# Opening of a two-layer encoder: modulation sums moved ahead of matrix products, one vector pass moved behind the low weights

## The chip, the cores and the metric

The kernel runs on one core of one Trainium2 chip. The metric is the time of one launch on the device, in microseconds (us); smaller is better. The engines of a core are TensorE (PE in the profile, with its weight loads as PEld), VectorE (DVE), ScalarE (ACT), GpSimd (POOL) and SyncE (SP), which here issues nearly all DMAs.

## The reference, cut to what matters

The whole computation is two layers of an encoder on 1024 tokens of width 1024 in float32. The change touches only what stands at the front of the first layer:

```
cond = jax.nn.silu(c)
mod = cond @ w_mod[l] + b_mod[l]
sh_a, sc_a, gt_a, sh_f, sc_f, gt_f = [m[:, None, :] for m in split_cols(mod, (D,) * 6)]
h = rms_norm(x, g_attn[l]) * (1 + sc_a) + sh_a
proj = h @ w_in[l]
```

Three groups of attention heads follow, an output projection, and a feed-forward part, all of it twice, and a last normalisation.

## The kernel before, in words

Products are made in "fp32r": a factor is split into a high part and a low part (`hh` and `hl` for the activations h, `whi` and `wlo` for weights), and three products high by high, low by high and high by low are added in PSUM. ACT makes the high part by a cast, DVE or POOL subtracts it to get the low part.

The width 1024 of h stands as eight chunks of 128 rows on the partitions, with the tokens along the free axis in two halves of 512. The opening (from line 816, `pin((pe, act, dve, sp), True)` among its first lines, up to the loop over the layers) works on the first half of the tokens in pairs of chunks. The attention part of `mod` (its columns for shift and scale) isn't ready beforehand: for each pair p it is made while the weights `w_mod` arrive, by the class `Mods`. Each pair reads two tiles `gm` of `w_mod`, rows 0 to 3 and rows 4 to 7 of eight blocks of 128 rows. The eight blocks are shared between two engines. DVE takes five or six of them (`m.add`), each as one multiply-add into the accumulator `ga` (128x512). PE takes the others directly (`m.col`), as four small matmuls of the gm block with the condition vector (`ps_m<-condT,gm`, 128x64; the profile counts each as two). `m.total(a)` then sums `ga` over the partitions with a column of ones (`ps_m<-onesr,ga`), for chunk a of the pair, and `m.finish(a)` lets DVE add the bias (`mod`) and form the scale (`gsc`). Only then can DVE scale the chunk (`nt`), ACT write its high part (`hh`), and DVE its low part (`hl`). For the first chunk of a pair in the first two pairs the scaling is done another way: `turned(n, rows)` multiplies the chunk of x by the row factors beforehand (`nt<-xt,rb`), and `h_turned` finishes it on ACT (`hh<-nt,mod,gsc`) and POOL (`ht`).

PE's main work beside this is `products(p, between)`: the chunks 2p and 2p+1 times the weights of the third head group (`wC`, loaded as `wst`, split by `w_high` on ACT and `low` on DVE), for four token blocks into four PSUM banks `ps_c`. It issues six passes of four 128x512 matmuls: high by high and high by low weights of the first chunk (`ps_c<-whi,hh`, `ps_c<-wlo,hh`), high by high of the second, low by high of both (`ps_c<-whi,hl`), and high by low weights of the second chunk. `between` is a list of functions, one called behind each pass. `a_first(u, q)` makes the chunks 2q and 2q+1 times the weights of the first head group (six matmuls `ps_ab`). `keep_busy(n)` issues n matmuls `ps_idle` that nobody reads, so that PE doesn't rest.

Loads of the opening go through SP's one queue in the order of the code: gm tiles (`gm_load`, three buffers), weight tiles `wst` (two buffers), blocks of x (`xn`). A load waits for its buffer, and those behind it wait with it.

What sets the order: within the opening PE, ACT, DVE and SP are pinned, so that each engine's instructions stand in the order in which the code calls them. POOL is not pinned, nor is what comes behind the opening: a scheduler places it. `skA<-skr`, a DMA that spreads a small bias table over 1 MB of device memory, belongs to that later part; its only reader here is `zv<-skA`, issued from 135.65 us on.

Of the kernel before, what the change touches and what calls it, by code (L numbers as in the profile page):

```python
# [76 lines left out]
def f32(ap):  # L77
    return ap.bitcast(F32)


def bc(ap, shape):
    return ap.to_broadcast(shape)
# [3 lines left out]
def trunk(ctx: ExitStack, tc, A, C, out):  # L86
# [115 lines left out]
    def mm3(ps, ah, al, bh, bl, first, last, **kw):  # L202
        pe.matmul(ps, ah, bh, start=first, stop=False, **kw)
        pe.matmul(ps, al, bh, start=False, stop=False, **kw)
        pe.matmul(ps, ah, bl, start=False, stop=last, **kw)
# [24 lines left out]
    def sub(out, a, b, eng=dve):  # L230
        eng.tensor_tensor(out=out, in0=a, in1=b, op=ALU.subtract)
# [328 lines left out]
    def x_load(half, j):  # L560
        t = stp.tile([P, D], F32, name="xn", tag="xn", bufs=4)
        r0 = half * H + j * P
        sp.dma_start(t, A["x"][0, r0 : r0 + P, :])
        return t

    def x_square(half, j, xn, r):
        junk = xt[:, 6:8, H:S]
        act.activation(
            junk, xn.rearrange("p (a b) -> p a b", a=2), AF.Square, accum_out=r[:, j : j + 1]
        )  # L570
# [43 lines left out]
    def turn_vecs(l, v):  # L614
        pst = psl.tile([P, 512], F32, name="pst", tag="mm")
        pe.transpose(pst[:, :72], v, ident[:72, :72])
        dve.tensor_copy(vecs[l], pst[:, :72])
# [5 lines left out]
    def gm_load(i, ks=(range(4),)):  # L623
        if i not in gms:
            gms[i] = stp.tile([P, 4, 2, 2 * P], F32, name="gm", tag="gm", bufs=3)
        for k in ks:
            r0 = (i % 2 * 4 + k.start) * P
            for g in range(2):
                c0 = g * 1024 + i // 2 * 2 * P
                rows = A["w_mod"][0, r0 : r0 + len(k) * P, c0 : c0 + 2 * P]  # L630
                sp.dma_start(
                    gms[i][:, k.start : k.stop, g, :], rows.rearrange("(k p) n -> p k n", p=P)
                )
# [55 lines left out]
    def turned(n, rows):  # L689
        t = stp2.tile([P, H], F32, name="nt", tag="nt", bufs=3)  # L690
        dve.tensor_tensor(out=t, in0=xt[:, n, 0:H], in1=rows, op=ALU.mult)
        return t

    def h_turned(n, xr):


        sh, sc = mods[0][:, n : n + 1], gsc[0][:, n : n + 1]
        act.activation(hh[:, n, 0:H], xr, AF.Identity, bias=sh, scale=sc)
        t = stp2.tile([P, H], F32, name="ht", tag="ht", bufs=1)
        pool.tensor_scalar(out=t, in0=xr, scalar1=sc, scalar2=sh, op0=ALU.mult, op1=ALU.add)  # L700
        return lambda: sub(hl[:, n, 0:H], t, f32(hh[:, n, 0:H]))

    def h_high(n, rows):
        t = stp2.tile([P, H], F32, name="nt", tag="nt", bufs=3)
        sh = mods[0][:, n : n + 1]
        dve.scalar_tensor_tensor(
            out=t, in0=xt[:, n, 0:H], scalar=gsc[0][:, n : n + 1], in1=rows,
            op0=ALU.mult, op1=ALU.mult,
        )
        act.activation(hh[:, n, 0:H], t, AF.Identity, bias=sh)  # L710
        return lambda: dve.scalar_tensor_tensor(
            out=hl[:, n, 0:H], in0=t, scalar=sh, in1=f32(hh[:, n, 0:H]),
            op0=ALU.add, op1=ALU.subtract,
        )

    def h_blocks(half, rows, ns, between=None):

        c = slice(half * H, (half + 1) * H)
        ts = {}
        for n in ns:  # L720
            t = ts[n] = stp2.tile([P, H], F32, name="nt", tag="nt", bufs=3)
            dve.scalar_tensor_tensor(
                out=t, in0=xt[:, n, c], scalar=gsc[0][:, n : n + 1], in1=rows,
                op0=ALU.mult, op1=ALU.mult,
            )
        for n, t in ts.items():
            act.activation(hh[:, n, c], t, AF.Identity, bias=mods[0][:, n : n + 1])
        for n, t in ts.items():
            dve.scalar_tensor_tensor(
                out=hl[:, n, c], in0=t, scalar=mods[0][:, n : n + 1], in1=f32(hh[:, n, c]),  # L730
                op0=ALU.add, op1=ALU.subtract,
            )
            if between:
                between()
                between = None

    def wc_stage(kp):
        st = stage()
        for dst, v in w_in_src(0, C_COLS, kp)(parts(st, 2)):
            sp.dma_start(dst, v)  # L740
        wcs.append(st)

    def c_first(n, passes=range(3)):

        wh, wl = wC[n // 2]
        first, last = n == 0, n == KC - 1
        for i in passes:
            h, w = ((hh, wh), (hl, wh), (hh, wl))[i]
            for t in range(T0):
                pe.matmul(  # L750
                    pssC[t], h[:, n, t * P : (t + 1) * P], w[:, n % 2],
                    start=first and i == 0, stop=last and i == 2, skip_group_check=True,
                )

    def products(p, between):

        n = 2 * p
        for a, i in ((n, 0), (n, 2), (n + 1, 0), (n, 1), (n + 1, 1), (n + 1, 2)):
            c_first(a, (i,))
            if between:  # L760
                between.pop(0)()

    def a_stage(u):
        ast.append(w_ab(0, EARLY_AB[u]))

    def a_high(u):

        st = parts(ast.pop(0), 2)
        hi, lo = (t[:, 6 - 2 * u : 8 - 2 * u, H:S] for t in (hh, hl))
        act.activation(hi, st, AF.Copy, scale=-0.125)  # L770
        return lambda: dve.scalar_tensor_tensor(
            out=lo, in0=st, scalar=-0.125, in1=f32(hi), op0=ALU.mult, op1=ALU.subtract
        )

    def a_first(u, p):

        for k in (2 * p, 2 * p + 1):
            n, c = 6 - 2 * u + k // 4, slice(H + k % 4 * P, H + k % 4 * P + P)
            mm3(
                pssA[u], hh[:, n, c], hl[:, n, c], hh[:, k, 0:H], hl[:, k, 0:H],  # L780
                k == 0, k == KC - 1,
            )
# [6 lines left out]
    def w_ab(l, oc):  # L789
        st = stage()  # L790
        c0 = oc * P if oc < 4 else 768 + (oc - 4) * P
        sp.dma_start(
            parts(st, KC), A["w_in"][l, :, c0 : c0 + P].rearrange("(k p) n -> p k n", p=P)
        )
        return st
# [23 lines left out]
    def keep_busy(n):  # L819

        for _ in range(n):
            pe.matmul(idle, identr, bc(identr[:, None, :], [P, 4, P]), start=True, stop=True)

    def w_high():
        st = wcs.pop(0)
        hi, lo = (wp.tile([P, 1024], F32R, name=n, tag="whl", bufs=8) for n in ("whi", "wlo"))
        wC.append((parts(hi, 2), parts(lo, 2)))
        act.copy(hi, st)
        return lambda: sub(lo, st, f32(hi))
# [32 lines left out]
    xr = [turned(0, rows)]  # L862
    rb = stp2.tile([P, H], F32, name="rb", tag="rb", bufs=2)
# [3 lines left out]
    m = Mods(0)  # L867
# [12 lines left out]
    first_low = next(lows)  # L880
    m.finish(0)
    low0 = h_turned(0, xr.pop(0))
    xr.append(turned(2, rb))
    m.total(1)
    m.finish(1)
    low1 = h_high(1, rb)
# [2 lines left out]
    second_low = next(lows)  # L889
    low1()  # L890
    second_low()
    gm_load(3)
    wc_stage(1)
    gm_load(4)
    a_stage(0)
    m = Mods(1)
# [3 lines left out]
    low()  # L900
    keep_busy(3)
    pssC = [psl.tile([P, 512], F32, name="ps_c", tag="mm") for _ in range(T0)]
    products(0, [lambda: None, lambda: None, lambda: m.col(3), lambda: None, lambda: m.col(6)])
    m.col(7)
    m.total(0)
    m.finish(0)
    low0 = h_turned(2, xr.pop(0))
    m.total(1)
    m.finish(1)
    low1 = h_high(3, rb)  # L910
    turn_vecs(1, v1)
    low0()
    low1()
    keep_busy(2)
    a_high(0)()
    gm_load(5)
    wc_stage(2)
# [4 lines left out]
    m = Mods(2)  # L922
    m.add(0, 1, 2)
    low = w_high()
    m.add(4, 5)
    low()
    m.add(6)
    pssA = [psl.tile([P, 512], F32, name="ps_ab", tag="mm") for _ in range(2)]
    products(1, [lambda: None, lambda: m.col(3)])
    a_first(0, 0)  # L930
    m.col(7)
    a_first(0, 1)
    m.total(0)
    m.total(1)
    m.finish(0)
# [2 lines left out]
    for j in (2, 3):  # L938
        xns[1].append(x_load(1, j))
    a_stage(1)  # L940
    h_blocks(0, rb, (4, 5))
    x_square(1, 0, xns[1][0], rxs[1])
    keep_busy(2)
    m = Mods(3)
    m.add(0, 1, 2)
    low = w_high()
# [24 lines left out]
    rb = stp2.tile([P, H], F32, name="rb", tag="rb", bufs=2)  # L971
# [37 lines left out]
    for l in range(2):  # L1009
# [861 lines left out]
        for n in range(-AHEAD - 1, N + 3):  # L1871
# [83 lines left out]
            m = n - 1 if n <= NC else n - 3  # L1955
# [572 lines left out]
        for u in range(NU):  # L2528
# [26 lines left out]
            if t < NB - 1:  # L2555
                continue
            m, half = {
                1: (0, 0), 2: (0, 0), 6: (0, 1), 7: (1, 1), 4: (1, 0), 5: (1, 1), 3: (0, 1),
            }[num]
# [25 lines left out]
        if last_layer:  # L2585
            blocks_ = [(1, j, nh) for j in range(4) for nh in range(2)]
            turned = [out_turn(*b) for b in blocks_[:7]]
# [106 lines left out]
```

## Time and profile before

| | before |
|---|---|
| median of three runs | 2370.83 us |
| the three runs | 2367.87, 2371.65, 2370.83 us |
| the profiled execution | 2369.28 us |
| its span, first to last instruction | 2367.5 us |
| mean granted TensorE clock over the span | 0.997 |
| PE busy | 2325.4 us |
| DVE busy | 1757.1 us |
| ACT busy | 1184.3 us |
| POOL busy | 778.0 us |

The profiled execution has a time of its own, 1.78 us over its span; sums from the trace are made against it. A row of the timeline has its start and its length in us, the engine, the operation, what it writes and reads, how many instructions were merged into it, and in brackets the idle time before it with what ended that. Starts on PE follow each other; the length of a matmul includes its way through the array, so that it overlaps the next one's start. A row of the stretches gives for each engine the busy time, then the clock granted to TensorE (1.00 is full), the share of the DMA engines' time and the bytes moved.

### The profile page before, as it was taken

What the parts mean: (1) busy time and instruction counts of PE and PEld (TensorE: products, weight loads), DVE (VectorE), ACT (ScalarE), POOL (GpSimd) and SP (SyncE); (2) the same over time, 40 slices, a digit from 0 to 9 for tenths busy, and PEclk for the clock granted to TensorE, in tenths of its full rate; (3) what the DMA queues carried; (4) which work ended last, traced back from release to release, by engine and by line L of the source; (5) the groups of instructions that cost most, each with busy time, mean ns of one, the idle gap of its engine ahead of it and who ended that gap; (6) DMA issues with size and microseconds to landing.
All of it is one profiled execution on the core that took longest, in us unless ns stands there. A gap on an engine that the chain in (4) does not pass through costs nothing.

```text
span 2367.5 us, 33491 instructions
## 1 busy us (share of the span) xinstructions
PE 2325.4 (98%) x11804; PEld 1959.8 (83%) x11804; DVE 1757.1 (74%) x2762; ACT 1184.3 (50%) x2262; POOL 778.0 (33%) x749
## 2 busy tenths in 40 slices
PE   9999999999999999999999999999999999999998
PEld 7888898888788888788888889988878888888886
DVE  6877998868867677595767689897796674537865
ACT  4423888845543333344633168896454434334443
POOL 1540446710344444100145124574005444430001
PEclk9999999999999999999999999999999999999999
DMA  8567406163445444785434861332634443339633
GB/s 290 172 204 222 135 21 195 46 214 98 130 137 165 156 138 151 218 244 173 155 102 134 245 186 28 92 103 96 216 98 134 154 149 103 98 109 291 213 120 112
DMA packets 307450, 358.02 MB, mean 151 GB/s; under 512 B 52029, under 2 KB 223901, under 8 KB 307281
## 3 DMA queue, kind: packets, MB, share of 16 engines
q1 hardware_dynamic: 290784, 346.26, 46.5%
q10 hardware_dynamic: 16128, 9.44, 1.5%
q8 instruction: 93, 1.52, 0.3%
q14 instruction: 77, 0.62, 0.1%
q0 software_dynamic: 368, 0.17, 0.0%
HBM read 270.84 MB, written 88.63 MB: 152 GB/s over the span
## 4 chain that ended last, share of the span: by engine, by line
PE 55%; DVE 5%; issue 4%; ACT 2%; DMA 2%; POOL 1%; SPq 0%; POOLq 0%; DVEq 0%; ACTq 0%
PE ps_w L49 23%; PE ps_d L49 15%; PE ps_o L49 4%; PE ps_ab L49 3%; PE pv L49 3%; PE T L49 2%; PE ps_v L49 2%; PE sC L49 2%; DMA wmt<-in_w_mod_dram 1%; DVE ws L49 1%; PE ps_c L49 1%; ACT pr L49 1%; DVE wpt L49 1%; DVE pt L49 0%; POOL ct L49 0%
## 5 line engine op out<-in xcount | busy, mean ns | idle before, releaser
L49 PE MATMUL ps_d<-wpt 128*128 128x512 f32 x1848 | 423.7, 390 | 1.0 <-ACT wpt L49 0.7
L49 PEld LDWEIGHTS ps_d<-wpt 128*128 128x128 f32 x1848 | 345.7, 188 | 74.3 <-issue 3.0
L49 POOL TENSOR_SCALAR pr<-pr,rs 128x1024 f32<-128x1024 f32 (+2 forms) x248 | 190.2, 781 | 186.3 <-DVE rs L49 168.9
L49 POOL TENSOR_TENSOR sg<-sg,u 128x512 f32<-128x512 f32 x82 | 118.4, 1445 | 347.7 <-ACT sg L49 221.6
L49 PE MATMUL pv<-pt,vs 128*128 128x256 f32 x1088 | 174.0, 296 | 14.2 <-DVE y L49 13.0
L49 ACT CAST wpt<-w 128x512 fp32r<-128x512 f32 x154 | 95.7, 621 | 182.2 <-PE ps_d L49 162.0
L49 DVE TENSOR_TENSOR pt<-T,pt 128x512 fp32r<-128x512 f32 x272 | 177.4, 679 | 7.1 <-ACT pt L49 5.7
L49 DVE SCALAR_TENSOR_TENSOR acc<-wmt,condT,acc 128x512 f32<-128x512 f32 (+1 forms) x98 | 115.9, 1189 | 79.9 <-DMA wmt<-in_w_mod_dram 79.4
L49 ACT CAST pt<-T 128x512 fp32r<-128x512 f32 x272 | 151.6, 585 | 42.4 <-PE T L49 41.0
L49 ACT COPY u<-ps_w 128x512 f32<-128x512 f32 x128 | 75.1, 587 | 192.9 <-PE ps_w L49 192.9
L49 POOL TENSOR_TENSOR wpt<-ws,wpt 128x512 fp32r<-128x512 f32 x80 | 111.1, 1390 | 181.5 <-ACT wpt L49 137.0
L49 DVE TENSOR_TENSOR wpt<-w,wpt 128x512 fp32r<-128x512 f32 x154 | 108.7, 706 | 81.3 <-ACT wpt L49 79.2
L49 PEld LDWEIGHTS pv<-pt,vs 128*128 128x128 f32 x1088 | 141.0, 189 | 27.0 <-DVE y L49 25.0
L49 PE MATMUL T<-identr,pr 128*128 128x128 f32 x1176 | 160.1, 273 | 0.8 <-DVE pt L49 0.4
L49 PEld LDWEIGHTS T<-identr,pr 128*128 128x128 f32 x1176 | 137.7, 140 | 15.8 <-issue 1.4
L49 ACT CAST wpt<-ws 128x512 fp32r<-128x512 f32 x176 | 107.7, 622 | 52.4 <-issue 23.0
L49 DVE TENSOR_TENSOR wpt<-graw,wpt 128x512 fp32r<-128x512 f32 x154 | 109.8, 713 | 16.6 <-ACT wpt L49 16.6
L49 DVE TENSOR_TENSOR wpt<-ws,wpt 128x512 fp32r<-128x512 f32 x96 | 82.5, 868 | 49.4 <-ACT wpt L49 49.1
L49 ACT CAST wpt<-graw 128x512 fp32r<-128x512 f32 x154 | 95.0, 617 | 46.9 <-DMA graw<-gpd 41.0
L49 DVE TENSOR_TENSOR ws<-wr 128x512 f32<-128x512 f32 x88 | 81.2, 923 | 49.9 <-POOL wpt L49 46.4
L49 DVE TENSOR_REDUCE rs<-sC 128x1 f32<-128x1024 f32 x88 | 107.4, 1220 | 12.4 <-PE sC L49 11.0
L49 PE MATMUL ps_w<-h22h,wpt 128*128 128x512 f32 x352 | 109.0, 391 | 2.7 <-ACT u L49 1.7
(310 smaller groups left out, 5937.1 us busy)
## 6 DMA issues: line engine op xcount, KB each, us to landing
wr<-in_w_gu_dram SPq DMA_DIRECT2D x92, 512.0 KB, 4.2
gpd<-sg SPq DMA_DIRECT2D x154, 256.0 KB, 4.3
graw<-gpd SPq DMA_DIRECT2D x76, 512.0 KB, 3.6
w<-in_w_down_dram SPq DMA_DIRECT2D x110, 256.0 KB, 5.0
wmt<-in_w_mod_dram SPq DMA_DIRECT2D x48, 512.0 KB, 5.7
qk<-qkd SPq DMA_DIRECT2D x44, 512.0 KB, 7.2
wst<-in_w_o_dram SPq DMA_DIRECT2D x32, 512.0 KB, 4.2
wmt<-in_w_mod_dram SPq DMA_DIRECT2D x64, 256.0 KB, 3.9
```

What stands on the lines that cost most here:

```text
L49: ins = op(*args, **kwargs)
```

## The change: what it does

Four things are rewritten in the opening of the first layer. The shared variable names below (`low0`, `low1`) are the functions that make the low parts later.

1. `turned(2, rb)` (one 128x512 multiply on DVE, `nt<-xt,rb`) leaves its place between the modulation sums of the first two chunks and stands behind the low part of the first weights.
2. In the first `products`, the last column (`m.col(7)`), both totals and both finishes are called behind the fifth pass instead of behind the sixth; `m.col(6)` moves one pass forward. One of the two `ps_idle` behind it is dropped.
3. For the pair of chunks 4 and 5, DVE's last row of the accumulator is added before the low weights are made, and both totals stand ahead of `a_first(0, 1)`.
4. The number of `ps_idle` ahead of the third `products` goes from two to three.

```diff
-    xr.append(turned(2, rb))
     m.total(1)
     m.finish(1)
     low1 = h_high(1, rb)
...
     second_low()
+    xr.append(turned(2, rb))
     gm_load(3)
...
-    products(0, [lambda: None, lambda: None, lambda: m.col(3), lambda: None, lambda: m.col(6)])
-    m.col(7)
-    m.total(0)
-    m.finish(0)
-    low0 = h_turned(2, xr.pop(0))
-    m.total(1)
-    m.finish(1)
-    low1 = h_high(3, rb)
+
+    def last_columns():
+        nonlocal low0, low1
+        m.col(7)
+        m.total(0)
+        m.finish(0)
+        low0 = h_turned(2, xr.pop(0))
+        m.total(1)
+        m.finish(1)
+        low1 = h_high(3, rb)
+
+    products(
+        0,
+        [
+            lambda: None, lambda: None, lambda: m.col(3), lambda: m.col(6), last_columns,
+            lambda: None,
+        ],
+    )
     turn_vecs(1, v1)
     low0()
     low1()
-    keep_busy(2)
+    keep_busy(1)
...
-    m.add(4, 5)
+    m.add(4, 5, 6)
     low()
-    m.add(6)
...
     a_first(0, 0)
     m.col(7)
-    a_first(0, 1)
     m.total(0)
     m.total(1)
...
     a_stage(1)
+    a_first(0, 1)
     h_blocks(0, rb, (4, 5))
     x_square(1, 0, xns[1][0], rxs[1])
-    keep_busy(2)
+    keep_busy(3)
```

How the rows stand on the engines follows; a difference has - for the order before and + for the order of the change.

On PE, in the first `products` (chunks 0 and 1, with the modulation of chunks 2 and 3 in `ps_m`):

```order
 L49 MATMUL ps_c<-whi,hh 128x512 x4
 L49 MATMUL ps_m<-condT,gm 128x64 x4
-L49 MATMUL ps_c<-whi,hl 128x512 x8
+L49 MATMUL ps_c<-whi,hl 128x512 x4
 L49 MATMUL ps_m<-condT,gm 128x64 x4
-L49 MATMUL ps_c<-wlo,hh 128x512 x4
+L49 MATMUL ps_c<-whi,hl 128x512 x4
 L49 MATMUL ps_m<-condT,gm 128x64 x4
 L49 MATMUL ps_m<-onesr,ga 128x64 x4
+L49 MATMUL ps_c<-wlo,hh 128x512 x4
 L49 MATMUL pst<-identr,v_150 128x72
-L49 MATMUL ps_idle<-identr 128x512 x2
+L49 MATMUL ps_idle<-identr 128x512
```

The totals (`ps_m<-onesr,ga`) moved ahead of the last pass `ps_c<-wlo,hh`, and one `ps_idle` is gone.

On PE, from the last column of the modulation of chunks 4 and 5 to the next `products`, before:

```order
L49 MATMUL ps_m<-condT,gm 128x64 x4
L49 MATMUL ps_ab<-hh 128x512
L49 MATMUL ps_ab<-hh,hl 128x512
L49 MATMUL ps_ab<-hl,hh 128x512
L49 MATMUL ps_ab<-hh 128x512
L49 MATMUL ps_ab<-hh,hl 128x512
L49 MATMUL ps_ab<-hl,hh 128x512
L49 MATMUL ps_m<-onesr,ga 128x64 x4
L49 MATMUL ps_idle<-identr 128x512 x2
L49 MATMUL ps_c<-whi,hh 128x512 x4
```

and in the change:

```order
L49 MATMUL ps_m<-condT,gm 128x64 x4
L49 MATMUL ps_m<-onesr,ga 128x64 x4
L49 MATMUL ps_ab<-hh 128x512
L49 MATMUL ps_ab<-hh,hl 128x512
L49 MATMUL ps_ab<-hl,hh 128x512
L49 MATMUL ps_ab<-hh 128x512
L49 MATMUL ps_ab<-hh,hl 128x512
L49 MATMUL ps_ab<-hl,hh 128x512
L49 MATMUL ps_idle<-identr 128x512 x3
L49 MATMUL ps_c<-whi,hh 128x512 x4
```

The six matmuls of `a_first(0, 1)` stood ahead of the totals and stand behind them now.

On SP, behind the last loads of the opening (`g` holds gains, `cst` rotary tables, `t` the bucket table; `xd<-xt` writes x back to device memory):

```order
-L49 DMA wst<-in_w_in_dram 128x8x128
-L49 DMA skA_91<-skr 512x1x512
-L49 DMA wst<-in_w_in_dram 128x8x128
+L49 DMA wst<-in_w_in_dram 128x8x128 x2
 L49 DMA g_532<-in_gq_ax_dram 128x6x64
 L49 DMA g_532<-in_gk_ax_dram 128x2x64
 L49 DMA cst<-const_rope_dram 128x128 x4
 L49 DMA t_544<-in_t_table_dram 32x6
+L49 DMA skA_91<-skr 512x1x512
 L49 DMA wst<-in_w_in_dram 128x8x128
```

The scheduler places the 1 MB `skA` behind the small tables now. Behind the opening no other row of any engine is moved.

## The prediction

> **What bounds the kernel now.** I read the busy times first, then the stretches around the change, then the timelines of PE and DVE there.
>
> ```profile
> PE 2325.4 (98%) x11804; PEld 1959.8 (83%) x11804; DVE 1757.1 (74%) x2762; ACT 1184.3 (50%) x2262; POOL 778.0 (33%) x749
> 41.45:43.77 2.32, 0.71 (x4) 0.28 (x3) 1.89 (x7) 0.77 (x2) 0.00 (x0) 1.00 1.10 381
> 43.77:48.10 4.33, 4.33 (x16) 3.63 (x17) 4.22 (x6) 4.30 (x7) 1.75 (x2) 0.61 0.83 264
> 90.00:150.00 60.00, 59.45 (x303) 48.93 (x302) 45.83 (x68) 23.54 (x53) 33.78 (x30) 1.00 0.56 153
> ```
>
> PE is busy 98% of the span, so a microsecond that PE gets back in the opening is worth a microsecond at the end, as long as nothing behind it is tied to something else: behind the opening (90 to 150 us) PE stands still for 0.55 us in 60. The opening has two visible losses. From 41.45 to 43.77 PE is busy for 0.71 us of 2.32, with `ps_idle` at that. From 43.77 to 48.10 PE is busy throughout, but its granted clock is 0.61 instead of 1.00: about 0.39 x 4.33 = 1.7 us of PE's work is lost to half clock. The DMA engines are full (share 1.10) in the first of these stretches, as in those ahead of it, so loads can't come earlier than they do.
>
> The timeline of PE, from the last pass of the first `products`:
>
> ```profile
> 26.71 1.17 PE L49 MATMUL ps_c<-wlo,hh 128*128 128x512 f32 x4
> 27.72 1.00 PE L49 MATMUL ps_m<-condT,gm 128*128 128x64 f32 x8
> 28.56 0.61 PE L49 MATMUL ps_m<-onesr,ga 128*128 128x64 f32 x4
> 29.42 0.66 PE L49 MATMUL ps_m<-onesr,ga 128*128 128x64 f32 x4 [0.26 <-DVE mod L49]
> 29.92 0.23 PE L49 MATMUL pst<-identr,v 72*128 72x72 f32 x1
> 29.95 0.71 PE L49 MATMUL ps_idle<-identr 128*128 128x512 f32 x2
> 30.50 1.17 PE L49 MATMUL ps_c<-whi,hh 128*128 128x512 f32 x4
> ...
> 33.24 1.17 PE L49 MATMUL ps_c<-whi,hh 128*128 128x512 f32 x4
> ...
> 38.36 1.00 PE L49 MATMUL ps_m<-condT,gm 128*128 128x64 f32 x8
> 39.17 0.48 PE L49 MATMUL ps_ab<-hh 128*128 128x512 f32 x1
> ...
> 40.64 1.00 PE L49 MATMUL ps_m<-onesr,ga 128*128 128x64 f32 x8
> 41.45 0.71 PE L49 MATMUL ps_idle<-identr 128*128 128x512 f32 x2
> 43.77 1.65 PE L49 MATMUL ps_c<-whi,hh 128*128 128x512 f32 x4 [1.61 <-ACT hh L49]
> ...
> 48.11 1.18 PE L49 MATMUL ps_c<-whi,hh 128*128 128x512 f32 x4
> ...
> 52.79 1.00 PE L49 MATMUL ps_m<-onesr,ga 128*128 128x64 f32 x8
> ```
>
> and that of DVE:
>
> ```profile
> 18.42 0.69 DVE L49 TENSOR_TENSOR nt<-xt,rb 128x512 f32<-128x512 f32 x1
> ...
> 19.26 0.50 DVE L49 SCALAR_TENSOR_TENSOR gsc<-mod,vecs 128x1 f32<-128x1 f32 x1
> ...
> 23.45 3.12 DVE L49 SCALAR_TENSOR_TENSOR ga<-gm,condT,ga 128x512 f32<-128x512 f32 x4
> 26.49 1.22 DVE L49 TENSOR_TENSOR wlo<-wst,whi 128x1024 fp32r<-128x1024 f32 x1
> 29.21 0.16 DVE L49 TENSOR_TENSOR mod<-ps_m,vecs 128x2 f32<-128x2 f32 x1 [1.50 <-PE ps_m L49]
> ...
> 30.32 0.20 DVE L49 SCALAR_TENSOR_TENSOR gsc<-mod,vecs 128x1 f32<-128x1 f32 x1
> ...
> 37.73 1.22 DVE L49 TENSOR_TENSOR wlo<-wst,whi 128x1024 fp32r<-128x1024 f32 x1
> 38.87 0.74 DVE L49 SCALAR_TENSOR_TENSOR ga<-gm,condT,ga 128x512 f32<-128x512 f32 x1
> 41.68 0.16 DVE L49 TENSOR_TENSOR mod<-ps_m,vecs 128x2 f32<-128x2 f32 x1 [2.07 <-PE ps_m L49]
> ...
> 43.76 1.42 DVE L49 SCALAR_TENSOR_TENSOR hl<-nt,mod,hh 128x512 fp32r<-128x512 f32 x2
> ...
> 50.45 0.75 DVE L49 SCALAR_TENSOR_TENSOR ga<-gm,condT,ga 128x512 f32<-128x512 f32 x1
> ```
>
> The reader is to see the round trip: totals on PE (28.56, 40.64), `mod` on DVE (29.21, 41.68), then scale, `hh` on ACT, and PE's next `products` (30.50, 43.77). The first trip takes 1.94 us and is just filled, partly with idle matmuls; the second takes 3.13 us and only 1.4 us of it is filled.
>
> **The change part by part.**
>
> *A, the first round trip.* The low pass, 27.72 - 26.71 = 1.01 us, goes behind the totals, so PE could begin them at 28.56 - 1.01 = 27.55. DVE holds this up. The moved `nt` (0.69 us) now stands ahead of `ga`, so the sums, which end at 23.45 + 3.12 = 26.57, end at 27.26: still in time. But the `wlo` cast behind them then ends at 26.49 + 0.69 + 1.22 = 28.40, and `mod` waits behind it on DVE, until 28.3 or so, for rows on DVE overlap by about 0.1; by PE alone it would be 27.55 + (29.21 - 28.56) = 28.20. So the trip starts 0.9 us earlier. Behind `mod` PE has the second total (starting 0.21 us after it, 0.50 us), the low pass (1.01), `pst` (0.03) and one idle matmul (half of 30.50 - 29.95, 0.28): the next `products` begins at 28.3 + 0.21 + 0.50 + 1.01 + 0.03 + 0.28 = 30.3, 0.2 us earlier. ACT's `hh` is ready well before, so PE's own work sets this. The other end: without `nt` in its old place the stage before may gain. There `gsc` took 0.50 us against 0.20 us in the next pair, in company with the POOL multiply; if those 0.3 us go, A is 0.5. The removed idle matmul is inside this sum. A gain beyond that I don't see, nor a loss: the `nt` multiply isn't asked for until ACT's `hh` of that chunk. I take **0.4** (0.2 to 0.5), since the long `gsc` stands next to the removed row.
>
> *B, the second round trip.* The totals move ahead of `a_first(0, 1)`, which takes 40.64 - 39.17 = 1.47 us. DVE's last sum (38.87, 0.74) now runs ahead of the `wlo` cast, at 37.73, and ends at 38.47, before PE asks at 39.17; the cast behind it ends at 39.7, before `mod` is asked at 39.17 + 1.04 = 40.21 (41.68 - 40.64). So the trip of 43.77 - 40.64 = 3.13 us starts at 39.17, and the next `products` could begin at 42.30. PE meanwhile has the totals (0.81), the six matmuls (1.47) and three idle ones (3 x 0.28 = 0.84): 3.12 us, so it arrives at 42.29. The wait of 1.61 goes, and nothing is left of it; the third idle matmul costs nothing, for the trip is as long. **B = 1.47**; if the idle matmuls or the trip run 0.1 long, 1.4.
>
> *C, the clock.* With no gap, the half clock behind it should go. From 43.77 to 48.11 PE made two passes, a column group and the start of the next pass; the same three groups took 33.24 - 30.50 = 2.74 us in the pair before. That is 4.34 - 2.74 = **1.60**. But DVE needs its time too: from `hl` at 43.76 to the end of the last sum, 50.45 + 0.75 = 51.20, it takes 7.44 us, and the totals at 52.79 need that sum. PE's way there is 52.79 - 43.77 = 9.02, less 1.60: 7.42. Both arrive together, so C is worth 1.60 and not more; a longer DVE row takes it back one for one. Bounds: 0 to 1.6.
>
> *D, the loads.* SP's gm load that waits for DVE's third row of pair 1 starts up to 0.6 us later, the one that waits for `col(7)` of that pair up to 1 us earlier. With the DMA share over 1.00 the queue is never empty, so neither moves a landing: 0. The 1 MB `skA` behind the small tables: 0 for PE, since its reader stands at 135.65 us; a price comes with the third rival.
>
> Sum: A + B + C = 0.4 + 1.47 + 1.60 = 3.47, against the profiled execution 2369.28 - 3.47 = 2365.8. That execution is 1.55 us faster than the median of the runs shown (2370.83), which lie between 2367.87 and 2371.65. The four times have a median of 2370.06; from that, 2366.6 us is my forecast.
>
> **The rivals.**
>
> *1. The gap goes, the clock doesn't count.* The stretch at half clock is in the one execution that was profiled; whether the timed runs have it, or the changed kernel gets one elsewhere, no row shows. Without C the totals of 52.79 would have come when DVE allows, at 51.2, so the change would give A + B = 1.87: 2370.06 - 1.87 = 2368.2. For it: the idle time was only 1.61 us, and the runs shown differ by 3.8 us, more than C, so some of them may well lack the slow stretch. Against it: the low clock begins within a microsecond of the gap's end, and a mean clock of 0.997 leaves room for little else of its kind. I give it a quarter.
>
> [...]
>
> *2. Loads set the pace.* PE and DVE ask up to 3.5 us earlier for data that can't land earlier. The last blocks of x are the tightest:
>
> ```profile
> 37.27 1.00 SPq L49 DMA_DIRECT2D xn<-in_x_dram  x2
> xn<-in_x_dram SPq DMA_DIRECT2D x2, 512.0 KB, 8.9
> 47.45 1.06 ACT L49 ACTIVATE xt<-xn 128x1024 f32<-128x1024 f32 x1
> ```
>
> Issued at about 37.3 and 37.8, with 8.9 us they land at about 46.2 and 46.7, and ACT reads the first at 47.45 - 1.9 = 45.6: 0.6 us of waiting, behind which nothing for `products(2)` stands on ACT. If it was a gm tile instead, C would shrink to about 0.6 and the time would be 2367.6; if it also held B, 2369.
>
> *3. Slower: the 1 MB behind the small tables.* The spills of x (`xd`) must have landed before `qk` is written over x.
>
> ```profile
> DMA packets 123, 0.25 MB, mean 84 GB/s; under 512 B 0, under 2 KB 0, under 8 KB 123
> 53.57 5.07 SPq L49 DMA_DIRECT2D g<-in_gq_ax_dram  x1
> g<-in_gq_ax_dram SPq DMA_DIRECT2D x1, 192.0 KB, 17.8
> g<-in_gq_ax_dram SPq DMA_DIRECT2D x1, 192.0 KB, 11.9
> 78.30 4.93 SPq L49 DMA_DIRECT2D xd<-xt  x8
> xd<-xt SPq DMA_DIRECT2D x1, 256.0 KB, 3.9
> 92.91 0.58 ACT L49 CAST qk<-pq 128x512 fp32r<-128x512 f32 x1
> ```
>
> `skA` alone moves at 84 GB/s (50.5 to 53.5 us), so its 1 MB takes some 12 us. Before, it ran under matmuls that need no load; now it runs behind `g`, among the spills. The last spill is issued by 83.2 and lands 3.9 us later, near 87; ACT needs it at 92.91, in the change at 89.4. `g` will be issued near 49 (an estimate: 53.57 less the opening's shift of 3.5 us, less the issue of `skA` that stood ahead of it). If it takes 17.8 us again, it lands at 67, `skA` ends at 79, then come 512 KB of weights (1.4 us at the 381 GB/s of the first stretch) and 16 spills at 4.93 / 8 = 0.62 each: 90.3, and ACT waits 0.9 us. It must wait past 92.9, its time before, for the kernel to end slower: that is the point, and a `skA` of 15 us reaches it; one of 17 us gives 2370.06 + 2 = 2372. Against it: in the second layer `g` lands after 11.9 us with no `skA` ahead of it (the second of its two landing times), which puts the last spill near 84.
>
> **How the numbers follow.** Forecast 0.62, at 2366.6. Rival 1 0.24, at 2368.2. Rival 2 0.10, at 2367.6 to 2369. Rival 3 0.04, at 2372. The forecast's own bounds are 2365.9 (A at 0.5 and some more from the shorter waits) to 2367; the shown runs spread by 3.8 us, so the range takes in 2 us to each side of the bounds: 2363.8 to 2370.0, which holds rivals 1 and 2. A measurement of this kernel can tell about 0.2%, 4.7 us, from no change. More than that needs 1.3 us beyond the sum, which the runs' spread gives to about a quarter of the forecast's cases and few of the others: faster 0.20, slower 0.04, within 0.2% 0.76.
>
> **What would show it.** In the changed profile: `ps_c` of chunk 2 at 30.0 to 30.3, no wait for ACT ahead of `ps_c` of chunk 4, which begins near 41.9; a granted clock of 1.00 from there on; the totals of pair 3 near 49.3 and the opening's last rows shifted by the same 3.5 us; spills that land before 89. Wrong would be: half clock again somewhere, totals that wait for `ga`, or ACT waiting ahead of `qk`.

## The result, and the profile after

| | before | after |
|---|---|---|
| median | 2369.74 us (22 runs, 2367.87 to 2371.65) | 2366.60 us (22 runs, 2364.41 to 2368.36) |
| the profiled execution, its span | 2367.5 us | 2365.0 us |

The ratio is 0.9987, with a 95% interval of 0.9981 to 0.9993: the change takes off 3.14 us, or 1.7 to 4.5. The forecast was 2366.6 us.

First the busy times, and the three stretches that the prediction showed of before, now of after (same columns):

```profile
PE 2324.0 (98%) x11804; PEld 1959.2 (83%) x11804; DVE 1758.8 (74%) x2762; ACT 1185.8 (50%) x2262; POOL 778.4 (33%) x749
41.45:43.77 2.32, 2.31 (x10) 1.61 (x9) 2.19 (x4) 2.32 (x5) 0.00 (x0) 1.00 1.09 377
43.77:48.10 4.33, 4.33 (x28) 3.85 (x27) 4.19 (x6) 3.86 (x6) 1.55 (x2) 1.00 0.82 262
90.00:150.00 60.00, 59.53 (x303) 48.93 (x302) 46.56 (x69) 22.33 (x50) 33.81 (x29) 1.00 0.60 166
```

Both losses of the opening are gone: PE is busy for 2.31 of 2.32 us where it had 0.71, and the clock behind is 1.00 where it was 0.61. The timeline of PE after, at the two round trips and the totals of pair 3:

```profile
21.16 1.20 PE L49 MATMUL ps_c<-wlo,hh 128*128 128x512 f32 x4 [0.25 <-DVE wlo L49]
...
27.59 0.61 PE L49 MATMUL ps_m<-onesr,ga 128*128 128x64 f32 x4
28.45 0.66 PE L49 MATMUL ps_m<-onesr,ga 128*128 128x64 f32 x4 [0.25 <-DVE mod L49]
28.92 1.17 PE L49 MATMUL ps_c<-wlo,hh 128*128 128x512 f32 x4
...
30.27 1.09 PE L49 MATMUL ps_c<-whi,hh 128*128 128x512 f32 x4
...
38.89 1.06 PE L49 MATMUL ps_m<-onesr,ga 128*128 128x64 f32 x8
...
41.23 0.85 PE L49 MATMUL ps_idle<-identr 128*128 128x512 f32 x3
42.08 1.20 PE L49 MATMUL ps_c<-whi,hh 128*128 128x512 f32 x4
...
48.59 1.09 PE L49 MATMUL ps_c<-wlo,hh 128*128 128x512 f32 x4
49.56 1.10 PE L49 MATMUL ps_m<-onesr,ga 128*128 128x64 f32 x8
```

and of DVE:

```profile
19.47 0.16 DVE L49 SCALAR_TENSOR_TENSOR gsc<-mod,vecs 128x1 f32<-128x1 f32 x1
...
27.03 1.22 DVE L49 TENSOR_TENSOR wlo<-wst,whi 128x1024 fp32r<-128x1024 f32 x1
28.24 0.16 DVE L49 TENSOR_TENSOR mod<-ps_m,vecs 128x2 f32<-128x2 f32 x1
...
48.76 0.75 DVE L49 SCALAR_TENSOR_TENSOR ga<-gm,condT,ga 128x512 f32<-128x512 f32 x1
```

The products of chunk 2 begin at 30.27 (forecast 30.3), those of chunk 4 at 42.08 without a wait (forecast 41.9), the totals of pair 3 at 49.56 (forecast 49.3). The `mod` of the first trip stands right behind the `wlo` cast with no idle time, and the last sum of pair 3 ends at 48.76 + 0.75 = 49.51, when PE's pass ahead of the totals (48.59, some 0.92 us) has just run out: DVE bounds the first place, and at the second both arrive together, as the working had it.

Starts in two executions can't be compared to a tenth, since the first product of the opening begins a little earlier or later each time (19.43 to 20.39 us in the profiles here). So I measure from the first `ps_c` to a matmul that follows the opening and waits for the same thing in all kernels (`ps_b`). The two rows of PE in before:

```profile
19.61 1.09 PE L49 MATMUL ps_c<-whi,hh 128*128 128x512 f32 x4
...
96.52 0.63 PE L49 MATMUL ps_b<-oneh,t5h 32*6 32x512 f32 x2 [0.23 <-DVE qko L49]
```

and in after:

```profile
19.83 1.08 PE L49 MATMUL ps_c<-whi,hh 128*128 128x512 f32 x4
...
93.33 0.62 PE L49 MATMUL ps_b<-oneh,t5h 32*6 32x512 f32 x2 [0.23 <-DVE qko L49]
```

That is 76.91 before and 73.50 after: **3.41 us less**, against a forecast sum of 3.47. In the first layer's attention the gain still stands. The same row of PE in before and in after is 336.95 and 333.57 us behind the first `ps_c`, 3.38 us apart:

```profile
356.56 1.49 PE L49 MATMUL T<-identr,pr 128*128 128x128 f32 x12
```

```profile
353.40 1.49 PE L49 MATMUL T<-identr,pr 128*128 128x128 f32 x12
```

Of the span only 2.5 us remained. Part of the rest shows in the waits of PE (us in total, times, longest), in the row for a load of the second layer, first of before, then of after:

```profile
PE sA L49 <- DMA qk<-qkd: 0.5, 1, 0.5
```

```profile
PE sA L49 <- DMA qk<-qkd: 1.6, 1, 1.6
```

In the other profiles of this study this wait is 0 to 0.8 us, in one of them (`sk_double`) 2.3 us, without a pattern in their openings. I take it for a difference between executions; no experiment tested it.

### The profile page after: what moved, and what is told of

The parts are those of the page before. It is cut to its first block, busy times and chain, and to the rows that moved or that the text cites. A ratio compares the mean times of both kernels' runs of the same rounds, so it can differ in the third digit from the quotient of the medians.

```text
span 2365.0 us, 33492 instructions
## 1 busy us (share of the span) xinstructions
PE 2324.0 (98%) x11804; PEld 1959.2 (83%) x11804; DVE 1758.8 (74%) x2762; ACT 1185.8 (50%) x2262; POOL 778.4 (33%) x749
```

## The experiments

The theory: A + B + C, with the half clock (C) caused by the pause of 1.61 us. Its main rival: A + B alone, since the half clock was seen in one profiled execution only. Times below are medians; "opening" is the stretch from the first `ps_c` to `ps_b`.

Each ratio is to runs of before on the same chip beside it.

| kernel | median us | ratio to before, 95% | opening us |
|---|---|---|---|
| before | 2369.74 | | 76.91 |
| `before_again` | 2370.44 | 0.9995 to 1.0013 | 75.54 |
| `gap_filled` | 2369.33 | 0.9989 to 1.0006 | 75.67 |
| `gap_long` | 2370.15 | 0.9994 to 1.0012 | 75.66 |
| `totals_a` | 2369.54 | 0.9992 to 1.0010 | 75.25 |
| `totals_b` | 2367.89 | 0.9985 to 1.0003 | 74.20 |
| after | 2366.60 | 0.9981 to 0.9993 | 73.50 |
| `nt_early` | 2366.44 | 0.9981 to 0.9999 | 73.86 |
| `no_idle` | 2367.03 | 0.9980 to 0.9997 | 73.62 |
| `sk_twice` | 2367.83 | 0.9979 to 0.9997 | 73.55 |
| `sk_double` | 2367.47 | 0.9983 to 1.0001 | 73.51 |
| `pass_behind` | 2366.22 | 0.9975 to 0.9992 | 72.58 |

The table is to be read with its row `before_again`: the unchanged kernel, run as if it were a change, came out 0.93 us above the kernel before beside it (2369.51). Differences under 1 us between medians say little here; the opening of the traces repeats to 0.13 us (75.54, 75.67 and 75.66 in three kernels whose edits only fill or empty the pause). The 76.91 of the first row is the one opening here with a stretch at half clock.

**Filling the pause.**

```diff
-    keep_busy(2)
+    keep_busy(8)
```

> The kernel before, with eight instead of two idle matmuls ahead of the third products, so that PE is busy from 41.45 to about 43.7 us (8 x 0.28 = 2.24) and nothing else moves. If the half clock comes from the 1.61 us of idle time (term C): the stretch 43.77 to 48.10 runs at 1.00, the totals of pair 3 start when DVE allows, at 51.2 instead of 52.79, and the kernel takes 1.6 us less than before, about 2368.1. If the clock has no part in the medians (rival 1): the time of before, 2369.7, whatever the one profile shows.

The stretches of this kernel, with the pause filled:

```profile
41.45:43.77 2.32, 2.09 (x11) 1.40 (x10) 1.92 (x7) 0.80 (x2) 0.00 (x0) 1.00 1.10 381
43.77:48.10 4.33, 4.33 (x23) 3.72 (x24) 4.22 (x6) 4.30 (x7) 1.77 (x2) 1.00 0.82 264
```

The clock is 1.00 and the totals of pair 3 begin at 51.22, both as C says. But the time is 0.5 us below before beside it, not 1.6. Taken alone, either theory could still hold.

**Parts 3 and 4 alone, and parts 1 and 2 alone.** The edits are those of the change's diff.

> Parts 3 and 4 alone. By the terms B and C: no wait for ACT ahead of the products of chunk 4, which begin at 42.3 us; full clock behind them; totals of pair 3 at about 49.7; 1.47 + 1.60 = 3.07 us less than before, about 2366.7. If the clock has no part: 1.47 less, about 2368.3. If the two moves of the change need each other: less than 1.5 us.

> Parts 1 and 2 alone. By the term A: the products of chunk 2 begin 0.2 to 0.4 us earlier, and everything behind them by as much, the 1.6 us of idle time and the half clock stay; 2369.3 to 2369.5. If A is worth what the sum lacks elsewhere: over 1 us. If it costs: over 2369.8.

`totals_b` shows no wait at chunk 4 and takes 1.94 us off the time, nearer to B alone (1.47) than to B + C (3.07), but its interval (0.7 us more to 3.6 us less) holds both. `totals_a` settled more than it was meant to: it keeps the wait of 1.61 us, and its clock is 1.00 behind it. So the pause by itself doesn't always bring the half clock. Parts A and B also aren't independent: A takes 0.29 us from the opening by itself (75.54 to 75.25) but 0.70 on top of B (74.20 to 73.50). In `totals_b` PE waits for DVE's last sum at the totals of pair 3. The row of DVE, then those of PE:

```profile
49.07 0.75 DVE L49 SCALAR_TENSOR_TENSOR ga<-gm,condT,ga 128x512 f32<-128x512 f32 x1
```

```profile
48.71 1.09 PE L49 MATMUL ps_c<-wlo,hh 128*128 128x512 f32 x4
49.87 1.10 PE L49 MATMUL ps_m<-onesr,ga 128*128 128x64 f32 x8
```

The sum ends at 49.07 + 0.75 = 49.82, and the totals start at 49.87. A pass like the one at 48.71 holds PE for 0.94 us (40.65 to 41.59 in `pass_behind`, below), so PE was free at 49.65 and waited 0.22 us.

The sum is late with one of the four `ga` rows ahead of it, the one that runs beside a copy of POOL. The four rows of DVE and the copy in `totals_b`:

```profile
44.02 3.99 DVE L49 SCALAR_TENSOR_TENSOR ga<-gm,condT,ga 128x512 f32<-128x512 f32 x4
45.62 1.05 POOL L49 COPY gm<-gm 8x465 f32<-8x465 f32 x1 [5.09 <-DMA gm<-in_rpb_na_dram]
```

The row that begins at 45.60 takes 1.63 us instead of 0.75. In after it takes 1.43, in `totals_a` 1.55 and in the second profile of before 1.43. In the profiles of all twelve kernels of the table, the row of `ga` that lies beside most of the copy ends 0.55 to 0.56 us behind the copy's end. So part A makes this row 0.12 us longer by itself and 0.20 us shorter on top of B, which is 0.32 of the 0.41 us between its two effects. No run moved the copy.

**A shorter pause.**

```diff
-    keep_busy(3)
```

> The changed kernel without the three idle matmuls ahead of the third products, so that PE stands still for about 0.85 us there and nothing else moves. If any such pause brings the half clock: a stretch at 0.6 behind it and 1.6 us more than the changed kernel, about 2368.2. If a pause of 0.85 us is too short: the time of the changed kernel, 2366.6, and a clock of 1.00. If it depends on where the pause falls in time: some executions with, some without, and a median between.

A wait of 0.69 us stands ahead of chunk 4, with a clock of 1.00 behind it, an opening 0.12 us longer and a time that can't be told from the changed kernel's. The three idle matmuls of the change neither cost nor gain.

**Before once more.** No edit.

> The kernel before, unchanged, as if it were a change: a second profile of it, and what such a measurement gives where nothing differs. If the half clock behind the 1.61 us of idle time is there in every execution: again 0.6 in that stretch. If it hangs on where the windows fall: more likely 1.00, with the totals of pair 3 at 51.2 to 51.5; a ratio within 0.0005 of 1.

The second profile of before has the same wait of 1.61 us (PE at 43.60) and the totals of pair 3 at 51.09 instead of 52.79. Why, shows when the stretches are cut at the places where the first profile's clock changes. It falls at 44.29 and comes back at 47.71, and it falls again at 2358.53, in the last microseconds. The half clock lasted 3.413 us, and (2358.53 - 44.29) / 678 = 3.4133 us: the two falls stand a whole number of the same step apart. Stretches of before, cut on that grid:

```profile
40.88:44.29 3.41, 1.80 (x11) 1.32 (x11) 2.41 (x7) 1.29 (x2) 0.35 (x1) 1.00 1.08 376
44.29:47.71 3.42, 3.42 (x12) 2.77 (x11) 3.35 (x5) 3.39 (x7) 1.39 (x2) 0.50 0.88 271
2355.12:2358.53 3.41, 2.08 (x16) 1.52 (x14) 1.76 (x5) 1.09 (x4) 0.00 (x0) 1.00 0.00 0
2358.53:2361.94 3.41, 0.00 (x0) 0.00 (x0) 2.70 (x5) 1.09 (x2) 3.40 (x3) 0.50 0.58 218
```

In the second profile the clock falls at 2361.10 at the end; 679 steps earlier lies 43.45:

```profile
40.03:43.45 3.42, 1.97 (x13) 1.45 (x11) 1.87 (x6) 0.62 (x1) 1.05 (x2) 1.00 1.09 366
43.45:46.86 3.41, 3.25 (x18) 2.87 (x19) 3.21 (x6) 3.41 (x6) 1.03 (x1) 1.00 1.05 345
2361.10:2364.51 3.41, 0.00 (x0) 0.00 (x0) 0.39 (x1) 0.00 (x0) 1.42 (x2) 0.50 1.02 378
```

In the first execution the window ahead of the half clock (from 40.88 on) took in the whole pause, 1.61 us of idle time, and 0.57 us of the small totals ahead of it; in the second, reckoned back from the fall at its end, the grid lay elsewhere, the pause was split by an edge at 43.45 with 1.45 us of idle time ahead of it, and the clock stayed at 1.00. So I take the clock in one such window to follow from what PE did in the window ahead of it, which the next two runs measure. In `totals_a` the same reckoning from the fall at the end (2360.69) gives an edge at 43.04, within its pause. The window 2355.12 to 2358.53 has only 1.33 us of idle time, with a clock of 0.50 behind it; its matmuls are small (128x128 and 128x1), which the runs below take up.

**How idle the window was.** A stretch of dense matmuls, then a pause, 84 times, at the front of the changed kernel.

```diff
     keep_busy(8)
+    for i in range(84):
+        keep_busy(28 + i * 7 % 13)
+        hops = (1, 2, 3, 5, 7, 9, 12)[i % 7]
+        dve.tensor_copy(pz[:, 0:1], idle[:, 0, 0:1])
...
+        dve.tensor_copy(pr[:, 0:1], pz[:, hops - 1 : hops])
+        pe.matmul(idle, identr, bc(pr[:, None, :], [P, 4, P]), start=True, stop=True)
```

> The changed kernel with a measurement of its own put into the opening: 84 stretches of 28 to 40 idle matmuls (about 6.5 to 9 us), each ended by a pause in which PE waits for a chain of tiny copies on DVE and ACT; seven chain lengths, twelve pauses of each, estimated at 0.6 to 4 us. Only the clock behind the pauses is of interest. If a pause of 1.6 us always brings the half clock: a sharp length below 1.6, with 12 of 12 above and 0 of 12 below. [...] If it depends on where the pause falls in time: a share between 0 and 12 that grows with the length, and at 1.6 us near a half, as the two profiles with that gap have it (one with, one without).

Pauses of 0.44 to 1.73 us: half clock behind none of 60. With nine copies in the chain, pauses of 2.14 us and a little more: behind 9 of 12; with twelve, of 2.77 us: behind 8 of 12. A pause of 1.73 us and one of 2.15 us in this kernel, each with the window that follows:

```profile
47.77:51.19 3.42, 1.69 (x7) 1.05 (x7) 0.78 (x5) 0.57 (x3) 0.00 (x0) 1.00 0.00 0
51.19:54.60 3.41, 3.41 (x17) 2.82 (x16) 0.00 (x0) 0.00 (x0) 0.00 (x0) 1.00 0.00 0
58.01:61.43 3.42, 1.27 (x6) 0.77 (x5) 0.93 (x6) 0.77 (x4) 0.00 (x0) 1.00 0.00 0
61.43:64.84 3.41, 3.41 (x10) 2.64 (x9) 0.00 (x0) 0.00 (x0) 0.00 (x0) 0.50 0.02 5
```

Sorted by the idle time inside one window, this run has no exception: no half clock behind any window with up to 1.73 us, half clock behind every one with 1.94 us or more. Both expectations of this run were wrong in part: by the pause the length isn't sharp (9 of 12 and 8 of 12), by the window it was.

**The round trip of before, repeated.** Four totals, two idle matmuls and a pause of 1.54 or 1.73 us (28 times each), or 1.95 us of pause alone (28 times).

```diff
+        if hops < 8:
+            for k in range(4):
+                pe.matmul(idle[:, k, 0:64], ident, bc(ones, [P, 64]), start=True, stop=True)
+            keep_busy(2)
```

> As the kernel with the pauses, but each of the 84 stretches ends like the second round trip of the kernel before: four products of 64 columns (eight rows of the profile), two idle matmuls, then a pause of about 1.5 us (28 times) or 1.7 us (28 times); the other 28 have a pause of about 1.95 us alone. By the windows that the first such kernel showed (3.41 us each on a fixed grid, half clock behind a window in which PE stood still for over 1.73 to 1.94 us): with the small products counted as partly idle, a fifth to a half of the 56 trips bring half clock, and those in which the window took in the products as well as the pause; none if the small products count as work. The pause alone: half clock in 0 to 13 of 28, as the bound lies at 1.94 or at 1.73. If C were in every execution of before: nearly all 56.

Half clock behind 7 of 28 trips with 1.54 us, 9 of 28 with 1.73 us, and 15 of 28 pauses of 1.95 us alone (0 to 13 were expected); the smallest idle time in a window that brought it was now 1.89 us, without small products. With 0.17 us or more of the small products in the window, 1.73 us was enough; with 1.54 us it took 0.81, and 0.43 was not enough. So the small products counted as idle in part in this run. The pause of before, 1.61 us, lies between the two, which lets one estimate half clock in **about 3 executions of 10** (16 of 56). One trip with its row of small products ahead, and its window with the next:

```profile
118.71 1.00 PE L49 MATMUL ps_idle<-onesr,identr 128*128 128x64 f32 x8
119.52 0.71 PE L49 MATMUL ps_idle<-identr 128*128 128x512 f32 x2
121.77 0.79 PE L49 MATMUL ps_idle<-pr__174,identr 128*128 128x512 f32 x1 [1.53 <-DVE pr__174 L49]
```

```profile
118.33:121.74 3.41, 1.90 (x13) 1.39 (x11) 0.62 (x4) 0.57 (x3) 0.00 (x0) 1.00 0.00 0
121.74:125.16 3.42, 3.39 (x8) 2.72 (x9) 0.00 (x0) 0.00 (x0) 0.00 (x0) 0.50 0.01 2
```

**A longer pause in before.**

```diff
-    keep_busy(2)
```

> The kernel before without the two idle matmuls ahead of the third products: the pause there grows from 1.61 to about 2.2 us and nothing else moves. If the half clock comes by chance and more often behind a longer pause: up to 0.7 us more in the mean than before (1.6 us in nearly all executions instead of in about half), 2369.9 to 2370.5, with a spread as wide as before. If the pause has no part in it: the time of before, 2369.8.

The pause is 2.13 us; the median rises by 0.33 us, which says nothing by itself. In the one profile the edge at 42.81 split the pause, the clock stayed at 1.00, and the opening is 75.66 us, against 75.54 in `before_again` with its pause of 1.61 us: without half clock the two differ by no more than openings repeat (0.13 us), and PE's wait there ends with ACT's `hh` in both.

**How often, by the clock of every execution.** The mean granted clock of each timed execution is known to 0.001. At the end of each of those twelve profiles the clock is at half for 6.6 to 10.0 us; with that alone the mean is 0.9979 or more, and one more window of 3.41 us lowers it by 0.0007. A mean of 0.997 thus marks an execution with such a window more, unless its end was over 11.8 us long, which no profile shows. An execution with such a window and a short end still reads 0.998, so the counts are on the low side.

| kernel | executions with 0.997 |
|---|---|
| before, beside the other kernels and as `before_again` | 18 of 98 |
| `totals_a` (pause 1.61 us) | 2 of 11 |
| `gap_long` (pause 2.13 us) | 5 of 11 |
| `gap_filled` | 0 of 11 |
| after | 3 of 22 |
| the six others without that pause | 1 of 66 |

This agrees with the pause as the cause: more often behind a longer pause, and 4 of 99 in the kernels without it (the last three rows). For before it gives a share of about 2 in 10 or more. What the window costs at the end of the kernel it doesn't settle: the 18 executions are 0.5 us slower than the other 80, which scatter by 1.4 us. The three of after are its slowest (2367.49 to 2368.36); where their clock was low, no profile shows.

**What A consists of.** The changed kernel with part 1 undone:

```diff
+    xr.append(turned(2, rb))
     m.total(1)
...
     second_low()
-    xr.append(turned(2, rb))
```

> The changed kernel with part 1 undone (the nt pass back between the first sums). By the term A: the first pair loses what the long gsc row costs (0.50 against 0.16 us), 0 to 0.3 us, while the low weights of the second pair come 0.69 us earlier and so the totals of pair 1 no longer wait for DVE: 0 to 0.7 us back. If part 1 is what A rests on: 0.2 to 0.3 us more than the changed kernel. If it costs: up to 0.4 us less. Either way within 2366.2 to 2367.0, so the trace has to tell.

The opening is 0.36 us longer. DVE and PE in this kernel:

```profile
19.79 0.50 DVE L49 SCALAR_TENSOR_TENSOR gsc<-mod,vecs 128x1 f32<-128x1 f32 x1
```

```profile
21.73 1.20 PE L49 MATMUL ps_c<-wlo,hh 128*128 128x512 f32 x4 [0.50 <-DVE wlo L49]
```

With the `nt` pass back, `gsc` takes 0.50 us again (0.16 after), and PE's wait for `wlo` is 0.50 instead of 0.25: of the 0.36 us, 0.25 stand in that wait. The median, 0.16 us lower, can't show it.

**The 1 MB behind the small tables.** First a second, unread copy; the scheduler put it in the place of `skA` and `skA` itself ahead of its readers, as the expectation says.

> The changed kernel with a second DMA of 1 MB, like skA and in its place among the small tables; skA itself then goes later, ahead of its readers. So the traffic in front of the spills is the same, and that in front of zv grows. If rival 3's margin is as the changed profile shows it (spills land 2.6 us before they are needed): no change, 2366.6. If the DMA at the later place holds the readers of skA and of the qk blocks: over 1 us more.

The opening is unchanged (73.55). The median is 1.23 us above the changed kernel's, measured beside other runs of before; with the 0.93 us of `before_again` that is inconclusive. The trace shows that `skA` in the later place does hold its reader: POOL begins with `zv` at 139.41 us instead of 137.22, behind the load. What of that reaches the end isn't shown. The other kernel makes the DMA twice as large in its place:

```diff
-    skA = [dp.tile([4, P, 512], F32, name=f"skA{l}") for l in range(2)]
+    sk0 = dp.tile([8, P, 512], F32, name="skA0")
+    skA = [sk0[0:4], dp.tile([4, P, 512], F32, name="skA1")]
...
+                sp.dma_start(sk0, bc(skr[:, None, :], [8, P, 512]))
```

> The changed kernel with a skA DMA of 2 MB instead of 1 MB in the same place (its second half is read by nobody). Rival 3 as a mechanism: at 84 to 100 GB/s it takes 11 to 12 us longer, the last spill lands near 98 instead of 87.2, ACT waits for it ahead of qk (89.7 in the changed kernel) for some 8 us, and the kernel loses 5 to 8 us, 2372 to 2375. If the spills pass it by on the other DMA engines: spills near 88, no wait, 2366.6.

No wait appears: ACT casts `qk` at 90.29 us, 0.58 us later than in after with an opening that began 0.56 us later (20.39), and the last spill lands at 88.29. The rate of the DMA explains it, over 1.6 us in which it runs alone, first in after (70.2 to 71.8 us), then here (66.2 to 67.8):

```profile
DMA packets 80, 0.16 MB, mean 102 GB/s; under 512 B 0, under 2 KB 0, under 8 KB 80
```

```profile
DMA packets 160, 0.33 MB, mean 205 GB/s; under 512 B 0, under 2 KB 0, under 8 KB 160
```

Twice the bytes ran at twice the rate, so the expectation, which let twice the bytes take twice the time, was wrong. The packets took 26.2% of the time of 16 DMA engines in after, as much as 4.2 engines, and 52.5% here, as much as 8.4. So the DMA of eight rows took twice as much of the DMA engines' time as that of four; why, no run here shows. Whether a late spill would slow the kernel wasn't tried, for this kernel didn't make one.

**One pass more behind the totals.** The same move as part 2, for the second products: their last pass goes behind the totals of pair 2 and takes the place of the three idle matmuls.

```diff
-    products(1, [lambda: None, lambda: m.col(3)])
-    a_first(0, 0)
...
-    keep_busy(3)
+    def totals_two():
+        a_first(0, 0)
...
+    products(
+        1,
+        [lambda: None, lambda: m.col(3), lambda: None, lambda: None, totals_two, lambda: None],
+    )
```

> The changed kernel, with the last pass of the second products moved behind the totals as well, in place of the three idle matmuls. The three (0.85 us) go from PE, the totals of pair 2 are asked 0.92 us earlier, at 38.0, when DVE's sums (37.6) are just done. If PE sets the pace there: products of chunk 4 at 41.2 instead of 42.08 and 0.85 us less than the changed kernel, 2365.7. If loads or DVE hold it (totals of pair 3 at 49.5 as before): 0 to 0.3 less.

PE in this kernel:

```profile
38.32 1.06 PE L49 MATMUL ps_m<-onesr,ga 128*128 128x64 f32 x8
...
40.65 1.09 PE L49 MATMUL ps_c<-wlo,hh 128*128 128x512 f32 x4
41.59 1.11 PE L49 MATMUL ps_c<-whi,hh 128*128 128x512 f32 x4
...
48.99 1.10 PE L49 MATMUL ps_m<-onesr,ga 128*128 128x64 f32 x8
```

The opening is 0.92 us shorter than after's (forecast 0.85) and keeps full clock. The median is 0.38 us below the changed kernel's; its interval against before (1.9 to 5.9 us less) doesn't part the two. In the opening it is the best of these kernels; at the end of its one profile nothing of that is left to see (span 2365.3 against 2365.0).

## Why the prediction was right, and where it was not

*What bounds the kernel.* Right: the two losses of the opening were real, and PE got back what it lost there.

*A.* Forecast 0.4 (0.2 to 0.5). At the products of chunk 2, where the working puts it, it measures (30.50 - 19.61) - (30.27 - 19.83) = 0.45. Its two sources were named rightly (the cast on DVE that bounds `mod`, the long `gsc` beside the POOL multiply), and the long `gsc` went as guessed. Over the whole opening it is 0.29 by itself and 0.70 on top of B. What the sum lacked is the `ga` row beside POOL's copy, which takes 1.32 to 1.63 us in the profiles and ends 0.55 to 0.56 us behind the copy.

*B.* Forecast 1.47. Measured in the opening: 1.34 by itself (75.54 to 74.20), 1.75 on top of A. A and B together give 75.54 - 73.50 = 2.04, where rival 1 had 1.87.

*C, the step that was mis-sized.* The mechanism was right: the profiled execution of before lost 76.91 - 75.54 = 1.37 us of its opening to the half clock, which stood behind a window with the pause (1.61 us) and 0.57 us of the small totals in it, and the change takes the pause away. At the totals of pair 3 it was (52.79 - 19.61) - (51.09 - 19.44) = 1.53 against the forecast 1.60; a little of it is made up before `ps_b`. Wrong was to put it in full against a median of runs. The half clock comes in some 2 to 3 executions of 10 (18 of 98 by the recorded clock, 16 of 56 trips), so in the mean it is worth 0.18 to 0.29 of 1.37, 0.25 to 0.4 us, and in most executions nothing. The sum for a typical run is thus 2.0, in the mean 2.3 to 2.4, and rival 1, given 0.24, describes more executions than the forecast does. Its remark that some of the runs "may well lack the slow stretch" is what the runs showed. The spread of the times, which the prediction took as a sign for that rival, is none: the runs of after spread just as wide (2364.41 to 2368.36).

*Why the number came out.* The base of the forecast, 2370.06, was 0.3 us above the median of 22 runs. The measured gain is 3.14 us, between 1.7 and 4.5; the traces account for 2.3 to 2.4. The 0.7 to 0.8 between them is less than what the unchanged kernel differed from itself (0.93). The medians can't tell the forecast's gain from that of rival 1, and that 2366.6 was met to the tenth is luck. Whether anything else lies in the 0.7 us stays open.

*D and rival 2, the loads.* Right: from the first `ps_c` on no load holds PE in the opening of after. The last two blocks of x, issued from 37.27 us on in before and from 36.30 on in after, took 8.9 and 9.6 us: asked earlier, they came no earlier. ACT waits 0.20 and 0.27 us for them (0.6 was priced), and the `rx` made from them comes in time. A load holds one of DVE's sums of pair 3 only in `pass_behind`, where DVE waits 0.15 us for a gm tile at 45.03.

*Rival 3.* The load of `g` and the cast of ACT in after:

```profile
g<-in_gq_ax_dram SPq DMA_DIRECT2D x1, 192.0 KB, 14.7
```

```profile
89.71 0.58 ACT L49 CAST qk<-pq 128x512 fp32r<-128x512 f32 x1
```

The load took 14.7 us, between the two values used, the last spill landed at 87.15, and the cast at 89.71 waited for nothing. The 12 us for `skA` were somewhat long: the stretch from which 84 GB/s was read (50.5 to 53.5 us) held the start of the transfer (nothing moved in its first 0.37 us), and at the 102 GB/s shown above 1.05 MB take 10.3 us.

## What to carry to other kernels

A pause on PE can cost more than itself: in one profile of before, half clock stood for 3.41 us behind a window that held the pause of 1.61 us and 0.57 us of small products, and the opening took 76.91 us; in the other the clock behind the same pause stayed at 1.00, and the opening took 75.54. Which of the two came differed from execution to execution (18 of 98 by the mean clock, 16 of 56 repeated trips), so such a loss belongs into the sum with its share and not in full. One profile doesn't show that share; the mean clock of many executions does. In this opening such waits were filled best with a pass that is due anyway, issued behind the request instead of ahead of it (72.58 us in `pass_behind` against 73.50 in after).

## What the runs showed of the hardware

- In the first profile of before the granted clock was at half for 3.413 us (44.29 to 47.71) and again from 2358.53 us on, two falls 678 steps of 3.4133 us apart. Reckoned back from the fall at the end in such steps, an edge lay at 43.45 us in the second profile of before, at 43.04 in `totals_a` and at 42.81 in `gap_long`, so the grid stood elsewhere in each execution.
- In `pauses` and `trips` (168 pauses in all), cut on such a grid, a window with up to 1.73 us of idle time and dense products around the pause never had half clock behind it, and one with 1.89 us and more always had; with products of 64 columns in the same window less was enough: 1.73 us with 0.17 us of such products, 1.51 us with 1.00 us of them.
- A DMA within device memory from four rows ran at 102 GB/s (`skA` in after) and one from eight rows at 205 GB/s (`sk_double`), each over 1.6 us in which it ran alone.
- POOL's operation `ht` of 128x512 took 1.13 us where DVE's multiply `nt` of 128x512 ran beside it, and DVE's 128x1 `gsc`, begun meanwhile, took 0.50 us and ended with it (six profiles). Without the multiply they took 0.76 and 0.16 us (six profiles).
- A 128x512 sum on DVE that began at or behind the start of POOL's 8x465 copy, or up to 0.02 us ahead of it, took 1.32 to 1.63 us instead of 0.75 and ended 0.55 to 0.56 us behind the copy (twelve profiles).
- The same kernel, measured against itself, gave a ratio of 1.0004 (0.9995 to 1.0013), 0.93 us between the medians of 11 and 27 runs.
